# A decoder trunk in float32: one more projection in seven products, and low parts made by adding transfers

## The chip, the cores and the metric

The kernel runs on one core of one Trainium2 chip. The metric is the device time of one execution in microseconds (us); lower is better.

## The reference

A small decoder trunk works on 512 tokens of width 1024 (T = 512, D = 1024) in float32. There are two layers. Each layer is a half-step SwiGLU FFN, a mixer, and a second half-step FFN, each with an RMSNorm ahead of it:

```python
x = x + 0.5 * swiglu(rmsnorm(x, g1), wg, wu, wd)   # FFN: D -> 2816 -> D
x = x + mixer(rmsnorm(x, g2))                      # layer 0: gated linear attention, layer 1: stick-breaking attention
x = x + 0.5 * swiglu(rmsnorm(x, g3), wg, wu, wd)

def swiglu(h, w_gate, w_up, w_down):
    return (silu(h @ w_gate) * (h @ w_up)) @ w_down
```

So there are four FFNs, each with three products of 1024 x 2816 weights. The change touches the FFNs alone.

## The kernel before

**Precision.** TensorE multiplies rounded numbers (fp32r). Each operand v is therefore split into a high part h (v rounded, a ScalarE copy) and a low part l = v - h (a VectorE subtraction), and each product is three matmuls: h·h, l·h and h·l. For weights this is done in `Entry.split` (lines 127 and 129: tiles `wh` and `wl`, made from the loaded tile `raw`, or `rawd` for down). For activations it is done in `cut` (lines 783 and 784).

**Entries and the feed.** The work of TensorE is a list of entries, which `Feed` plays in order. When an entry starts, the weights of it and of the next two are split, the views of the next three are made (a view may compute sums of weight blocks), and the loads of the next five are issued on SyncE's queue. Within that, the instructions of each engine go out in the order in which they were scheduled at build time, and each engine works in that order. Weight tiles `wh` and `wl` have four buffers, `raw` has two, `rawd` has two, and the banks of the accumulator memory are eight.

**An FFN.** The 2816 hidden columns are 11 chunks of 256. Gate and up of a chunk are done in one of two ways. In the plain way (`feat`), an entry makes 128 columns out of 8 blocks of the input, with 24 matmuls of 512 columns. In the other way (`seven`), a chunk of 256 columns is made by a Strassen-like scheme over 2 x 2 halves, with seven products in place of eight: each is 12 matmuls of 256 columns, in two entries (`body_1`, `body_2`, line 689). It needs sums of weight blocks (`s12` and `s34`, lines 672 to 679), sums of input blocks T (`ts`, line 793, made in `normed_input` and split by `sums` into `th` and `tl`), and copies of partial sums out of the accumulators by ScalarE (z, o0, o1 and u3, lines 713 to 731), from which VectorE goes on. In every FFN chunk 0 and chunk 1 go the plain way in gate and in up, and chunks 2 to 10 are done with seven products.

**Down.** The chunks are in groups, and the down product of a group is done while the next group's gate and up run. A plain `down` entry takes 24 matmuls of 512 columns and adds into x from the accumulator (line 323, VectorE). One group of two chunks has its down done in seven products too (`seven_down`, line 368). There the accumulators are also read by VectorE's adds into x (line 374); the bank of the third product t3 goes on to take t4, after the add has read it.

**Start of an FFN.** The FFN begins before its RMSNorm is known: its first entries work on the gained but not normalised x, and their evacuations multiply by R, the reciprocal norm (lines 823 and 830). When R is known (lines 533 or 556), VectorE makes the normalised input (`xn`, `nl`, `ts`) in four pieces spread over the next entries; `NORMED` says from which entry on it is used. Then `sums` splits the eight sums T in pieces, which must be there before the first `seven`. The constants of this order are:

```python
GROUPS = ((0, 2), (2, 4), (4, 6), (6, 8), (8, 9), (9, 11))
NORMED, SEVEN, AHEAD = 6, 2, 2
DOWN_SEVEN = (1,)
SEVEN_UP = (2, 3, 4, 5, 6, 7, 8, 9, 10)
```

So ahead of the first `seven` there are eight plain entries (gate and up of chunks 0 and 1) and two of the four downs of group 0.

**GpSimd** has no part in the FFNs. It issues a few small loads for the mixers and the load of the last norm's gain.

Of the kernel before, what the change touches and what calls it, by code (L numbers as in the profile page):

```python
# [10 lines left out]
F32 = mybir.dt.float32  # L11
# [4 lines left out]
ALU = mybir.AluOpType  # L16
# [16 lines left out]
def decoder(ctx: ExitStack, tc: tile.TileContext, a: dict, out: bass.AP):  # L33
# [61 lines left out]
    class Entry:  # L95
# [3 lines left out]

        def __init__(self, units, body, place=0, lead=False):  # L100
            self.units, self.body, self.W, self.place = units, body, None, place
            self.lead, self.views = lead, None

        def view(self):

# [4 lines left out]
        def split(self):  # L110
            if self.W is None:
                self.W = []
                for r, (_, _, n, m) in zip(self.view(), self.units):
                    few = n * m < 1024
                    if few:

                        h = st["few"].tile([P, n * m + NEAR], F32R, tag="vh", bufs=1, name="wh")[:, NEAR:]
                        l = st["few"].tile([P, n * m + 64 - NEAR], F32R, tag="vl", bufs=1, name="wl")[:, : n * m]
                    else:
                        h, l = (  # L120
                            wp.tile([P, n * m + 64], F32R, tag="w" + t, bufs=4, name="w" + t)[
                                :, self.place : self.place + n * m
                            ]
                            for t in "hl"
                        )
                    h, l = (t.rearrange("p (n m) -> p n m", m=m) for t in (h, l))
                    st["cut"] = nc.scalar.copy(h, r).ins  # L127
                    with tc.issue_after(st["gains"]):
                        nc.vector.tensor_tensor(out=l, in0=r, in1=h.bitcast(F32), op=ALU.subtract)  # L129
                    self.W.append((h, l))  # L130
                    if self.lead and len(self.W) == 1:

                        first = wp.tile([P, P], F32R, tag="w1", bufs=1, name="w1")
                        nc.scalar.copy(first, r[:, 0, 0:P])
                        self.first = first
# [158 lines left out]

                feed.q.append(Entry([u], body))

    def down(w, r0, nf, hs, part, nxt, late=0):


        nd = KD // nf  # L300
        src = w[r0 : r0 + nf * P, part * nd * P : (part + 1) * nd * P]
        ch = Chunk(src.rearrange("(f p) c -> p f c", p=P), nf, nd * P)
        ch.few = True

        def body(W):
            (wh, wl), = W
            acc = []

            def prod(m, fs):
                if m == len(acc):  # L310
                    acc.append(psum("ps_d"))
                s = slice(m * P, (m + 1) * P)
                for f in fs:
                    mm3(acc[m], wh[:, f, s], wl[:, f, s], hs[f][0], hs[f][1], f == 0, f == nf - 1)

            if late:
                for m in range(nd):
                    prod(m, range(nf - late))
            for m in range(nd):
                prod(m, range(nf - late if late else 0, nf))  # L320
                ps = acc[m]
                k = part * nd + m
                nc.vector.scalar_tensor_tensor(  # L323
                    out=xs[k], in0=ps, scalar=0.5, in1=xs[k], op0=ALU.mult, op1=ALU.add
                )
                if nxt is not None:
                    nxt(k)
                yield

        feed.q.append(Entry([(ch, lambda t: t, nf, nd * P)], body))  # L330

    def seven_down(pool, w, r0, hs, part):

# [69 lines left out]
        def body_2(W):  # L403
            s, a22 = W
            ws, qs = v["w"], v["q"]
            for m in range(2):
                prod(ws[m], s, 0, 1, m, "t3", False)
                add(m, 1, 1, ws[m])
            yield
            for m in range(2):  # L410
                prod(qs[m], s, 2, 1, m, "b22", False)
                add(m, 0, 1, qs[m])
            yield
            for m in range(2):
                prod(ws[m], a22, 0, 1, m, "t4", False)
                add(m, 1, 0, ws[m])
            yield
# [168 lines left out]
    class FFN:  # L586
# [3 lines left out]

        GROUPS = ((0, 2), (2, 4), (4, 6), (6, 8), (8, 9), (9, 11))
        NORMED, SEVEN, AHEAD = 6, 2, 2
        DOWN_SEVEN = (1,)
        SEVEN_UP = (2, 3, 4, 5, 6, 7, 8, 9, 10)

        def __init__(self, wg, wu, wd, gi, nxt, first=False, last=False):
            self.gi, self.normed = gi, False
            self.after_ffn = bool(phases) and isinstance(phases[-1], FFN)  # L600
            self.defer, self.gates = [], []
            self.lead = []
            self.hs = [[] for _ in self.GROUPS]
            base, downs, late = len(feed.q), [], []
            self.sums_by = 10**6
            for group, (c0, c1) in enumerate(self.GROUPS):
                slots, put = 2 * (c1 - c0), 0
                if group == 1:

                    for put in range(self.AHEAD):  # L610
                        down(*downs[put], late=put == 0)
                    put = self.AHEAD
                for i in range(slots):
                    c, f = c0 + i // 2, i % 2
                    if f == 0:
                        g, u = Chunk(cols(wg, c * 256, 256), KD, 256), Chunk(cols(wu, c * 256, 256), KD, 256)
                    d = self.defer if i == 0 and c == 0 else None
                    f_ = f
                    if first and c == 0:

                        g, u = (Chunk(cols(w, f * P, P), KD, P) for w in (wg, wu))
                        self.lead += [g, u]
                        f_ = 0
                    if c >= self.SEVEN:
                        if f == 0:
                            self.sums_by = min(self.sums_by, len(feed.q) - base)
                            self.seven(g)
                    elif c not in self.SEVEN_UP:
                        feat(g, f_, self.evac_g, defer=d)
                    elif f == 0:  # L630
                        feat(g, 0, self.evac_g), feat(g, 1, self.evac_g)
                        self.sums_by = min(self.sums_by, len(feed.q) - base)
                    if c not in self.SEVEN_UP:
                        feat(u, f_, lambda ps, h=group: self.evac_u(ps, h), defer=d)
                    elif f == 1:
                        self.seven(u, group)

                    if late and i == 0:
                        seven_down(*late.pop())
                    while c >= self.SEVEN and put < len(downs) * (i + 1) // slots:  # L640
                        down(*downs[put])
                        put += 1
                    if group - 1 in self.DOWN_SEVEN and i == 1:
                        args = (lambda: self.tp, wd, self.GROUPS[group - 1][0] * 256, self.hs[group - 1])
                        seven_down(*args, 0)
                        late.append((*args, 1))
                for x in downs[put:]:
                    down(*x)
                n = 2 * (c1 - c0)
                end = group + 1 == len(self.GROUPS)  # L650
                downs = [(wd, c0 * 256, n, self.hs[group], part, nxt if end else None) for part in range(n)]
                if group in self.DOWN_SEVEN:
                    downs = []
            self.count = len(feed.q) - base
            if last:
                back_tok(wd, c0 * 256, n, self.hs[group], nxt)
            else:
                for x in downs:
                    down(*x)
            self.total = len(feed.q) - base  # L660
# [149 lines left out]
        def sums(self):  # L810
            def piece(i):

                h = np_.tile([P, T], F32R, tag="xh", name="th")
                l = np_.tile([P, T], F32R, tag="xl", name="tl")
                self.ts[i] = self.cut(h, l, self.ts[i].rearrange("p a b -> p (a b)"))


            return [lambda i=i: piece(i) for i in (0, 1, 2, 4, 6, 3, 5, 7)]
# [58 lines left out]
        def run(self, between=None):  # L877
            with tc.tile_pool(name="hp", bufs=8, reuse_waits="tile") as self.hp, tc.tile_pool(
# [20 lines left out]
                self.normed = True  # L899
                st["h"], st["l"] = zip(*self.n)  # L900
                todo = self.sums()
                spread(todo[:5], self.sums_by - self.NORMED)
                feed.entries(1, True)
                for piece in todo[5:]:
                    piece()
                feed.entries(self.count - self.sums_by - 1, True)
                if between is not None:
                    with tc.issue_after(st["silu"]):
                        nc.scalar.preload_act_table_set("sqrt_and_others")
# [681 lines left out]
```

## Time and profile before

| | |
|---|---|
| median of 3 runs | 1854.52 us (1854.33 to 1854.69) |
| the profiled execution, its own time | 1856.01 us |
| its span in the profile | 1854.0 us |
| granted TensorE clock | 0.999 |
| TensorE matmul, busy | 1828.8 us, 99%, 12187 matmuls |
| VectorE, busy | 1476.4 us, 80% |
| ScalarE, busy | 1035.9 us, 56% |
| GpSimd, busy | 8.7 us |

In the profile PE is TensorE's matmul, PEld its weight load, DVE VectorE, ACT ScalarE, POOL GpSimd and SP SyncE. A row of a group gives the source line, the engine, the operation, the tiles written and read, the shape, the count, the busy time, the mean duration in ns, and the idle time of the engine just before, with what ended it. A row of the timeline or of the chain gives the start in us, the length in us, the engine and the line. A row of waits gives who waited for whom, the total in us, how often and the longest.

### The profile page before, as it was taken

Reading aid. Unit: us, or ns where it says so; the run is one execution under the profiler, and the core shown is the slowest. Engines: PE = TensorE matmul, PEld = TensorE weight load, DVE = VectorE, ACT = ScalarE, POOL = GpSimd, SP = SyncE. Lnnn points to the kernel's source line nnn. Section 1 sums busy time; section 2 is a strip of 40 time slices with the busy share of each in tenths; the row PEclk is TensorE's granted clock in tenths of the full one; section 3 lists DMA queues with packets and bytes.
Section 4 is the critical chain, followed back from the end, with each engine's and each line's share of the span. In section 5 each row is a group of like instructions: output and inputs, shape, how many; then the busy total and the mean of one; then the engine's idle time right before and its main releaser. Section 6 shows DMA issues by size and latency. Waiting matters only on the chain.

```text
span 1854.0 us, 29888 instructions
## 1 busy us (share of the span) xinstructions
PE 1828.8 (99%) x12187; PEld 1649.6 (89%) x12187; DVE 1476.4 (80%) x2336; ACT 1035.9 (56%) x1771; POOL 8.7 (0%) x20
## 2 busy tenths in 40 slices
PE   7999999999999999999999999999999999999998
PEld 6999999889888899999889999998888788999997
DVE  7998776785787989877798997676878779997775
ACT  6555445444555565545565555455878755654454
POOL 0000000100000000000000000000000000000000
PEclk9999999999999999999999999999999999999999
DMA  5333333311223223332233333232221222333321
GB/s 160 114 125 95 118 110 100 98 57 62 69 69 114 91 92 115 115 114 87 82 128 104 98 118 107 95 92 85 69 69 59 67 91 93 112 125 97 121 80 69
DMA packets 177613, 179.16 MB, mean 97 GB/s; under 512 B 4098, under 2 KB 167988, under 8 KB 177476
## 3 DMA queue, kind: packets, MB, share of 16 engines
q1 hardware_dynamic: 176768, 176.18, 30.1%
q8 instruction: 95, 1.56, 0.4%
q0 software_dynamic: 608, 1.05, 0.2%
q14 instruction: 42, 0.34, 0.1%
q10 hardware_dynamic: 100, 0.03, 0.0%
HBM read 175.17 MB, written 2.10 MB: 96 GB/s over the span
## 4 chain that ended last, share of the span: by engine, by line
PE 86%; DVE 9%; DMA 3%; ACT 2%; issue 1%; SPq 0%; DVEq 0%; ACTq 0%
PE ps_d L67 20%; PE ps_f L67 18%; PE ps_w L689 17%; PE ps_q L689 9%; PE ps_t L67 5%; PE ps_z L689 4%; PE ps_b L67 4%; DVE wl L129 3%; DMA raw<-in_ffn_w_gate_dram 2%; PE ps_S L67 1%; PE ps_z L1315 1%; PE ps_bt L67 1%; PE ps_oT L1377 1%; PE ps_w L368 1%; DVE x L374 1%
## 5 line engine op out<-in xcount | busy, mean ns | idle before, releaser
L129 DVE TENSOR_TENSOR wl<-raw,wh 128x1024 fp32r<-128x1024 f32 (+1 forms) x244 | 259.2, 1066 | 89.3 <-ACT wh L127 50.1
L127 ACT CAST wh<-raw 128x1024 fp32r<-128x1024 f32 (+1 forms) x244 | 224.7, 923 | 160.4 <-PE ps_d L67 45.4
L689 PE MATMUL ps_w<-th,wh 128*128 128x256 f32 x864 | 239.6, 277 | 1.4 <-ACT o L719 0.6
L689 PE MATMUL ps_w<-tl,wh 128*128 128x256 f32 x864 | 238.7, 276 | 0.0
L689 PE MATMUL ps_w<-th,wl 128*128 128x256 f32 x864 | 238.6, 276 | 0.0
L129 DVE TENSOR_TENSOR wl<-s,wh 128x1024 fp32r<-128x1024 f32 x160 | 195.4, 1222 | 54.0 <-PE ps_z L689 37.4
L127 ACT CAST wh<-s 128x1024 fp32r<-128x1024 f32 x160 | 168.0, 1050 | 116.8 <-PE ps_d L67 28.9
L67 PE MATMUL ps_d<-hh,wl 128*128 128x512 f32 x544 | 212.1, 390 | 0.0
L67 PE MATMUL ps_d<-hh,wh 128*128 128x512 f32 x544 | 212.1, 390 | 0.0
L67 PE MATMUL ps_d<-hl,wh 128*128 128x512 f32 x544 | 211.6, 389 | 0.0
L67 PE MATMUL ps_f<-xh,wh 128*128 128x512 f32 x448 | 178.9, 400 | 1.6 <-ACT wh L127 1.6
L67 PE MATMUL ps_f<-xl,wh 128*128 128x512 f32 x448 | 175.8, 393 | 0.0
L67 PE MATMUL ps_f<-xh,wl 128*128 128x512 f32 x448 | 175.1, 391 | 0.0
L689 PEld LDWEIGHTS ps_w<-th,wh 128*128 128x128 f32 x864 | 162.3, 188 | 3.0 <-ACT u L731 1.0
L689 PEld LDWEIGHTS ps_w<-th,wl 128*128 128x128 f32 x864 | 162.2, 188 | 0.0
L689 PEld LDWEIGHTS ps_w<-tl,wh 128*128 128x128 f32 x864 | 162.2, 188 | 0.0
L127 ACT CAST wh<-rawd 128x1024 fp32r<-128x1024 f32 (+1 forms) x84 | 84.9, 1012 | 120.3 <-PE ps_d L67 77.4
L323 DVE SCALAR_TENSOR_TENSOR x<-ps_d,x 128x512 f32<-128x512 f32 x152 | 102.9, 688 | 58.6 <-PE ps_d L67 58.0
L129 DVE TENSOR_TENSOR wl<-rawd,wh 128x1024 fp32r<-128x1024 f32 (+1 forms) x84 | 98.3, 1174 | 42.4 <-ACT wh L127 25.1
L67 PEld LDWEIGHTS ps_d<-hl,wh 128*128 128x128 f32 x544 | 102.1, 188 | 21.6
L67 PEld LDWEIGHTS ps_d<-hh,wh 128*128 128x128 f32 x544 | 102.1, 188 | 20.2
L67 PEld LDWEIGHTS ps_d<-hh,wl 128*128 128x128 f32 x544 | 102.1, 188 | 19.7
(323 smaller groups left out, 4847.9 us busy)
## 6 DMA issues: line engine op xcount, KB each, us to landing
raw<-in_ffn_w_gate_dram SPq DMA_DIRECT2D x43, 1024.0 KB, 5.4
raw<-in_ffn_w_up_dram SPq DMA_DIRECT2D x43, 1024.0 KB, 5.4
rawd<-in_ffn_w_down_dram SPq DMA_DIRECT2D x84, 512.0 KB, 3.7
raw<-in_gla_w_in_dram SPq DMA_DIRECT2D x12, 1024.0 KB, 5.3
raw<-in_sb_w_in_dram SPq DMA_DIRECT2D x16, 512.0 KB, 3.8
raw<-in_gla_w_out_dram SPq DMA_DIRECT2D x4, 1024.0 KB, 5.0
raw<-in_sb_w_in_dram SPq DMA_DIRECT2D x4, 1024.0 KB, 5.1
raw<-in_sb_w_out_dram SPq DMA_DIRECT2D x4, 1024.0 KB, 5.0
```

Of the source, the lines that this page charges most:

```text
L67: st["pe"] = nc.tensor.matmul(ps, l, r, start=first, stop=last).ins
L127: st["cut"] = nc.scalar.copy(h, r).ins
L129: nc.vector.tensor_tensor(out=l, in0=r, in1=h.bitcast(F32), op=ALU.subtract)
L323: nc.vector.scalar_tensor_tensor(out=xs[k], in0=ps, scalar=0.5, in1=xs[k], op0=ALU.mult, op1=ALU.add)
L368: st["pe"] = nc.tensor.matmul(ps, l_, r_, start=first and c + n == 0, stop=c == 1 and n == 2, skip_group_check=True).ins
L374: nc.vector.scalar_tensor_tensor(out=x, in0=ps, scalar=0.5, in1=x, op0=ALU.mult, op1=ALU.add)
L689: st["pe"] = nc.tensor.matmul(o, l_, r_, start=first and j + n == 0, stop=j == 3 and n == 2, skip_group_check=True).ins
L1315: nc.tensor.matmul(o_, l_, r_, start=first, stop=last, skip_group_check=True)
L1377: nc.tensor.matmul(po[e * 64 : e * 64 + 64, j * P : T], self.v[j][:, c : c + 64], self.wt[p, e][bk][:, c0 : c0 + n], start=j == 0, stop=j ...
```

## The change

1. Up of chunk 1 is done with seven products (`SEVEN_UP` from 1 on). Its gate stays plain.
2. The groups' borders move from 2, 4, 6, 8, 9 to 1, 3, 5, 7, 9. The group of a single chunk is now chunk 0, not chunk 8, and the group whose down is done in seven products is chunks 3 and 4, not 2 and 3.
3. Both downs of chunk 0 stand between the two plain gate entries of chunk 1. Ahead of the first `seven` there are now five plain entries, the two downs and one more plain entry. The four pieces of the normalised input are spread over three entries, not four, and the eight pieces of T's splitting over the three entries after that (six) and just ahead of the first `seven` (two).
4. The low part of these two downs' weights and of T is made without VectorE: ScalarE writes -v into the tile of l, rounded as h is, and a transfer on GpSimd's queue adds v to it, which leaves v - h.
5. In the seven-product down, ScalarE copies the accumulator after t3 into a tile `u3`, and VectorE adds into x from the copy.

```diff
@@ Entry.split
                     st["cut"] = nc.scalar.copy(h, r).ins
+                    if self.adds:
+
+                        nc.scalar.activation(l, r, AF.Copy, scale=-1.0)
+                        nc.gpsimd.dma_start(out=l, in_=r, accum_op=ALU.add)
+                        self.W.append((h, l))
+                        continue
                     with tc.issue_after(st["gains"]):
                         nc.vector.tensor_tensor(out=l, in0=r, in1=h.bitcast(F32), op=ALU.subtract)
@@ down: adds=False as a new argument, at the end
         feed.q.append(Entry([(ch, lambda t: t, nf, nd * P)], body))
+        feed.q[-1].adds = adds
@@ seven_down, body_2
+            u3 = pool().tile([P, 2, H], F32, tag="c", bufs=1, name="u3")
             for m in range(2):
                 prod(ws[m], s, 0, 1, m, "t3", False)
-                add(m, 1, 1, ws[m])
+                nc.scalar.copy(u3[:, m], ws[m])
+                add(m, 1, 1, u3[:, m])
@@ FFN
-        GROUPS = ((0, 2), (2, 4), (4, 6), (6, 8), (8, 9), (9, 11))
-        NORMED, SEVEN, AHEAD = 6, 2, 2
-        DOWN_SEVEN = (1,)
-        SEVEN_UP = (2, 3, 4, 5, 6, 7, 8, 9, 10)
+        GROUPS = ((0, 1), (1, 3), (3, 5), (5, 7), (7, 9), (9, 11))
+        NORMED, SEVEN = 5, 2
+        DOWN_SEVEN = (2,)
+        SEVEN_UP = (1, 2, 3, 4, 5, 6, 7, 8, 9, 10)
@@ FFN.__init__
-                if group == 1:
-
-                    for put in range(self.AHEAD):
-                        down(*downs[put], late=put == 0)
-                    put = self.AHEAD
...
                     elif f == 0:
-                        feat(g, 0, self.evac_g), feat(g, 1, self.evac_g)
+                        feat(g, 0, self.evac_g)
+
+                        for put, x in enumerate(downs):
+                            down(*x, late=put == 0, adds=True)
+                        downs = []
+                        feat(g, 1, self.evac_g)
                         self.sums_by = min(self.sums_by, len(feed.q) - base)
@@ FFN.sums
-                self.ts[i] = self.cut(h, l, self.ts[i].rearrange("p a b -> p (a b)"))
+                t = self.ts[i].rearrange("p a b -> p (a b)")
+                nc.scalar.copy(h, t)
+
+                nc.scalar.activation(l, t, AF.Copy, scale=-1.0)
+                nc.gpsimd.dma_start(out=l, in_=t, accum_op=ALU.add)
+                self.ts[i] = h, l
@@ FFN.run
-                spread(todo[:5], self.sums_by - self.NORMED)
-                feed.entries(1, True)
-                for piece in todo[5:]:
+                spread(todo[:6], self.sums_by - self.NORMED)
+                for piece in todo[6:]:
                     piece()
-                feed.entries(self.count - self.sums_by - 1, True)
+                feed.entries(self.count - self.sums_by, True)
```

More of the change, by code (lines that the diff above doesn't have):

```diff
@@ L101, in __init__ @@
             self.units, self.body, self.W, self.place = units, body, None, place
-            self.lead, self.views = lead, None
+            self.lead, self.views, self.adds = lead, None, False
         def view(self):
@@ L295, in back, with down @@
                 feed.q.append(Entry([u], body))
-    def down(w, r0, nf, hs, part, nxt, late=0):
+    def down(w, r0, nf, hs, part, nxt, late=0, adds=False):
         nd = KD // nf
```

## The prediction

> **What bounds the kernel now.** I read the page first (busy shares, then the chain that ended last), then the chain in order of time for the spacing of the matmuls, then the waits.
>
> ```profile
> span 1854.0 us, 29888 instructions
> PE 1828.8 (99%) x12187; PEld 1649.6 (89%) x12187; DVE 1476.4 (80%) x2336; ACT 1035.9 (56%) x1771; POOL 8.7 (0%) x20
> PE 86%; DVE 9%; DMA 3%; ACT 2%; issue 1%; SPq 0%; DVEq 0%; ACTq 0%
> ```
>
> TensorE is busy for 99% of the span and owns 86% of the chain. Since ends of matmuls are modelled, I check it by starts. The next rows are from the chain in order of time: start, length, what, how many; the two before them give the shapes.
>
> ```profile
> L67 PE MATMUL ps_f<-nh,wh 128*128 128x512 f32 x64 | 24.9, 389 | 0.0
> L689 PE MATMUL ps_w<-th,wl 128*128 128x256 f32 x864 | 238.6, 276 | 0.0
> 290.88 2.72 PE ps_w L689 x24
> 353.50 10.88 PE ps_f L67 x48
> 598.79 34.98 PE ps_f L67 x154
> 633.77 10.88 PE ps_d L67 x48
> ```
>
> The 24 products of 256 columns take 2.72 us, 113.3 ns each, and the 48 of 512 columns take 10.88 us, 226.7 ns each: the same price per column, with starts so close that "mean ns of one" (276, 389) is overlap. In the second FFN the plain products run on for 34.98 us without a pause and the down products follow at once. So here TensorE's work is the time, almost to the last microsecond, and what is taken from it is gained. The Trainium skill ("Trainium Kernel Development and Optimization", Performance Expectations, Reading a trace) says that matmul busy time tells badly how near a kernel is to its limit and that the share of weight loading tells better. By that rule the 89% would leave 11% that better feeding could win; the even spacing of the starts speaks against it here, and the sum below goes by the starts.
>
> What is left of waiting inside the FFNs is in the waits of TensorE and of its weight loads: us in total, times, longest.
>
> ```profile
> PE ps_w L368 <- DVE x L374: 5.4, 8, 1.1
> PE ps_w L689 <- ACT o L719: 0.6, 1, 0.6
> PE ps_w L689 <- ACT u L731: 0.4, 2, 0.2
> PE ps_w L689 <- ACT ps_z L713: 0.4, 2, 0.2
> PEld ps_w L368 <- DVE x L374: 7.2, 9, 1.3
> ```
>
> **Edit 1, chunk 1's up in seven products.** Each of the four FFNs gives up two plain up entries, 48 products of 512 columns, 10.88 us. It gains 7 x 4 x 3 = 84 products of 256 columns, 84 x 113.3 ns = 9.52 us. That is 1.36 us less per FFN and 5.4 us in all, on the engine that sets the time. Nothing else of TensorE's work changes: the group of one chunk, with its eight sums into x, moves from chunk 8 to chunk 0, and the number of down products stays.
>
> **Edit 2, the sum in down copied by ScalarE.** After the t3 product, TensorE needs the bank again for t4, and VectorE has to have read it. VectorE stands in a long subtraction then, so TensorE waits: 5.4 us in eight places, one for each half of each FFN's seven-product down (7.2 us as the weight loads see it). The seven products of gate and up do already what the edit does, and the wait on their copy (u, L731) is 0.4 us over 72 of them. So the gain is bounded by 7.2 us and by nothing at all, if VectorE's lateness only comes out at the next operand that it has to make. I take 5.4 us: VectorE keeps its adds, but none of them stands between two products any more, and the copies lie on ScalarE, at 56%.
>
> **Edit 3, the order.** Group borders are now 1, 3, 5, 7, 9. The last two chunks get four downs between their sevens where they had two, and the seven-product down comes after two chunks with a down behind every seven. Both give VectorE more TensorE time to hide behind. The waits that could go are 0.6 + 0.4 + 0.4 = 1.4 us; I take half, 0.7 us, with 0 and 1.4 as ends.
>
> **Edit 4, the start of each FFN, where the price lies.** So far eight plain entries and two downs stood ahead of the first seven (in the second FFN it starts at 633.77 + 10.88 = 644.65). Now eight entries do (five plain, two downs, one plain), so it starts 10.88 us earlier after the same beginning, at 633.8. The normalised input and the sums T must be ready by then. The windows show what VectorE has to spare: us, then busy time of PE, PEld, DVE, ACT.
>
> ```profile
> 600.00:610.00 10.00, 10.00 (x46) 8.26 (x45) 9.10 (x16) 7.13 (x10) 0.00 (x0) 1.00 0.00 0
> 610.00:620.00 10.00, 10.00 (x46) 8.29 (x45) 10.00 (x21) 6.51 (x11) 0.00 (x0) 1.00 0.01 2
> 620.00:630.00 10.00, 10.00 (x46) 8.24 (x45) 10.00 (x17) 8.02 (x15) 0.00 (x0) 1.00 0.46 137
> 630.00:640.00 10.00, 10.00 (x46) 8.29 (x45) 9.93 (x15) 2.29 (x4) 0.00 (x0) 1.00 0.56 179
> 640.00:650.00 10.00, 10.00 (x70) 9.22 (x69) 10.00 (x15) 4.06 (x6) 0.00 (x0) 1.00 0.34 105
> 30.00:40.00 10.00, 10.00 (x46) 8.28 (x45) 10.00 (x20) 6.03 (x9) 0.00 (x0) 1.00 0.00 2
> 938.00:948.00 10.00, 10.00 (x46) 8.29 (x45) 10.00 (x20) 7.46 (x10) 0.00 (x0) 1.00 0.00 0
> 1529.00:1539.00 10.00, 10.00 (x46) 8.29 (x45) 10.00 (x20) 6.81 (x11) 0.00 (x0) 1.00 0.00 1
> ```
>
> VectorE has nothing to spare: 49 of 50 us, and the same at that place in the other three FFNs, though no wait of TensorE comes of it yet. So I count what must be done in the shorter time. VectorE's instructions overlap, and the timeline gives the distance of their starts:
>
> ```profile
> 602.25 0.69 DVE L556 SCALAR_TENSOR_TENSOR R<-v,R 128x512 f32<-128x512 f32 x1
> 602.86 1.22 DVE L129 TENSOR_TENSOR wl<-raw,wh 128x1024 fp32r<-128x1024 f32 x1
> 605.19 1.41 DVE L777 SCALAR_TENSOR_TENSOR xn<-x,gT,R 128x512 f32<-128x512 f32 x2
> 606.51 0.42 DVE L793 TENSOR_TENSOR ts<-xn 128x256 f32<-128x256 f32 x1
> 608.65 0.69 DVE L784 TENSOR_TENSOR hl<-t,hh 128x512 fp32r<-128x512 f32 x1
> 609.26 0.42 DVE L793 TENSOR_TENSOR ts<-xn,ts 128x256 f32<-128x256 f32 x1
> 609.59 0.42 DVE L793 TENSOR_TENSOR ts<-xn 128x256 f32<-128x256 f32 x1
> 644.73 1.23 DVE L129 TENSOR_TENSOR wl<-s,wh 128x1024 fp32r<-128x1024 f32 x1
> 645.87 0.68 DVE L673 TENSOR_TENSOR s<-s,raw 128x512 f32<-128x512 f32 x1
> ```
>
> A 512-wide one costs 0.60 (608.65 to 609.26), a 256-wide one 0.33, a 1024-wide one 1.14, a pair of xn 1.32. R is there at 602.9. The second product of the first seven, which reads T and s12, comes at 633.77 + 1.36 = 635.1, so VectorE has 32.2 us. Its list: the low part in hand 1.14; chunk 0's eight evacuations 4.8; four normalised pieces, each 1.32 + 2 x 0.60 + 4 x 0.33 = 3.84, 15.4; the first gate of chunk 1, 0.6; the low parts of the two plain gate entries 2.3; two sums and two low parts for the seven 3.5; eight sums of the downs into x, 4.8. Together 32.5 us. It fits to within 0.3 us, but only because T's eight low parts (4.8) and those of the two downs (2.3) have left VectorE: with them the list is 39.6 us, and TensorE would stand still for 7 us in each FFN. What can be late next is any pause of VectorE in that list: the windows show 0.9 us of pause at its head. I take 0.5 us per FFN, 2 us in all; the ends are nothing, where a few of the downs' sums slip behind the seven, and 3 us per FFN, 12 us.
>
> **Edit 5, the transfers that add.** The low part is now -t written by ScalarE, and a transfer on GpSimd's queue that adds t: ten more ScalarE passes per FFN (8 at 0.62, 2 at 1.05: 7.1 us on an engine that is busy for 28 of these 50 us) and ten transfers. Nothing of before adds in a transfer; the nearest rows are plain ones of that queue; rows of VectorE and ScalarE stand with them:
>
> ```profile
> lf<-in_c_lvl_dram POOLq DMA_DIRECT2D x1, 224.0 KB, 2.7
> fin<-in_final_norm_dram POOLq DMA_DIRECT2D x1, 512.0 KB, 4.1
> 332.12 1.95 POOL L988 DMA_DIRECT2D w<-in_gla_w_gk_dram  x4
> 332.90 1.23 DVE L129 TENSOR_TENSOR wl<-rawd,wh 128x1024 fp32r<-128x1024 f32 x1 [0.36 <-ACT wh L127]
> L783 ACT CAST th<-ts 128x512 fp32r<-128x512 f32 x32 | 17.8, 616 | 0.3 <-DVE ts L793 0.3
> L127 ACT CAST wh<-s 128x1024 fp32r<-128x1024 f32 x160 | 168.0, 1050 | 116.8 <-PE ps_d L67 28.9 <-DVE s L679 26.9 <-PE ps_q L689 20.4
> ```
>
> Four were issued in 1.95 us, so ten cost GpSimd some 5 us, and it has no other work in an FFN. For T's 256 KB I bound the landing from below by 2.7 us (224 KB) and from above by 8.2, twice the 512 KB row, since an add must read its target too; I take 4, near that row itself. If T's last two pieces are written about 626, where the windows above still have VectorE full, ScalarE needs 4 x 0.62 = 2.5 us and the transfer 4: 632.5. The piece read last among the even ones is needed at 635.1 + 0.9, the odd ones at the fifth product, 639.2. So 3.5 us are over, and I cost the edit at nothing. That cover is gone from 7.5 us of landing on; at the upper bound it would cost 0.7 us per FFN, 2.8 us in all, which the range holds. Behind a late transfer stand the tiles it reads, which VectorE's next sums for the sevens reuse, and the weight buffer's next load on SP's queue. The Trainium skill ("SBUF — State Buffer", summary rules) advises against hiding a GpSimd-issued transfer under VectorE, because making its descriptors starves while VectorE runs in a two-port mode. By that rule the issues would stretch by the subtractions beside them, up to 1.2 us each. The trace does not agree for these subtractions: the one at 332.90 ran beside the four issues, which kept 0.49 us each.
>
> **The sum.** 5.4 + 5.4 + 0.7 - 2.0 = 9.5 us less. The profiled execution took 1856.01 us, so 1846.5; it lay 1.5 us above the median of the runs (1854.52), which gives 1845.0.
>
> **Rivals.** (a) Slower: the transfers come one behind another instead of overlapping. First T pieces leave ScalarE about 611 (the first sums are done at 609.6); eight at 4.1 us land by 644, against the 636 allowed: 8 us per FFN, 32 in all, and the total is 1845.0 + 32 = 1877. The gain is gone once the wait per FFN exceeds (9.5 / 4) = 2.4 us, that is from (636 - 611 + 2.4) / 8 = 3.4 us for each transfer. For it: no row shows an adding transfer, and issues held up by VectorE would act the same way. Against: the four small ones overlapped. Chance 0.18. (b) VectorE's start of the FFN costs its upper end, 12 us: 10 us later than forecast, 1855, no change. For it: full windows. Against: the list fits. Chance 0.07. (c) Edit 2 does not do what it says, since VectorE's lateness comes out elsewhere: 5.4 us less gain, 1850.4; with (b) half true it is 1852 or more. Chance 0.13, of which half ends within the bound below. (d) All goes well: 5.4 + 7.2 + 1.4 = 14 us less, 1840.5. Chance 0.10. The forecast, between 1841 and 1850, has 0.52.
>
> **How the numbers follow.** A measurement of this kernel can tell 0.2%, 3.7 us, from no change. Faster: forecast, (d) and half of (c), 0.68. Same: (b) and the rest of (c), 0.14. Slower: (a), 0.18. The range goes from 1840 (d) to 1855 (b) and leaves out (a); the forecast's own range is 1841 to 1850.
>
> **What would show it.** TensorE's products of 512 columns fall by 4 x 48 and those of 256 rise by 4 x 84; the wait of ps_w (L368) on VectorE's x vanishes, with a small one on the new copy; the first seven of each FFN starts 10.9 us sooner after its R. Wrong would be: waits of TensorE on tl or on a transfer there (then a), on wl or nl (then b), or on wl in the seven-product down (then c).

## The result and the profile after

The changed kernel takes 1864.92 us (median of 6 runs, 1863.49 to 1869.16) against 1854.61 us for the kernel before beside it (6 runs): 1.006 of the time before, 95% interval 1.0047 to 1.0072. That is 10.3 us slower, where 9.5 us faster had been forecast. The profiled execution took 1866.02 us, its span 1864.2 us.

The page of the kernel after, its rows of busy time, the chain's shares, and two groups of TensorE by form:

```profile
span 1864.2 us, 30434 instructions
PE 1830.6 (98%) x12331; PEld 1657.3 (89%) x12331; DVE 1467.4 (79%) x2332; ACT 1075.1 (58%) x1859; POOL 43.2 (2%) x60
PE 86%; DVE 8%; DMA 4%; ACT 2%; issue 1%; SPq 0%; DVEq 0%; ACTq 0%
L67 PE MATMUL ps_f<-nh,wh 128*128 128x512 f32 x32 | 12.4, 389 | 0.0
L699 PE MATMUL ps_w<-th,wl 128*128 128x256 f32 x912 | 252.5, 277 | 0.0
```

TensorE has 144 matmuls more and is still at 98%, so this part of the page does not show what happened. Counted by form over the whole trace, those of 256 columns went from 7648 to 7984 (+336) and those of 512 from 3734 to 3542 (-192): at 113.3 and 226.7 ns that is 5.4 us less work. The span grew by 10.2 us all the same, so TensorE stood still for longer. The waits say at whom (us in total, times, longest):

```profile
PE ps_w L699 <- ACT ps_z L723: 6.8, 7, 2.3
PE ps_w L699 <- ACT u L741: 5.5, 7, 1.7
PE ps_q L375 <- ACT o L709: 3.2, 2, 1.7
PE ps_w L375 <- ACT ps_z L393: 0.2, 1, 0.2
ACT wh L127 <- DVE s L689: 23.9, 5, 6.4
DVE s L688 <- DMA tl<-ts: 7.4, 3, 2.5
DVE s L682 <- DMA raw<-in_ffn_w_gate_dram: 17.5, 19, 1.9
ACT w L140 <- DMA raw<-in_ffn_w_up_dram: 13.6, 8, 2.7
```

The 5.4 us that TensorE waited for VectorE's x in the seven-product down are gone. In their place it waits for small ScalarE copies (z, u, o), and these are only the last link: ScalarE waits for VectorE's sums, and VectorE for a transfer (`tl<-ts`) and for weight loads.

To place the stalls I add up, entry by entry, how far the starts of TensorE's matmuls are apart beyond 113.3 ns or 226.7 ns each. Two places hold them: the start of each FFN, up to the end of its first four projections in seven products (two entries each), and the stretch, the six entries from the first to the last one of the seven-product down.

| us of stall, four FFNs together | before | after |
|---|---|---|
| the start | 1.3 | 13.0 |
| the stretch | 10.8 | 13.7 |

**The start.** In the second FFN of the kernel after, the timeline of GpSimd, SyncE, VectorE, ScalarE and TensorE (start, length, what, and the idle time before it with its cause):

```profile
626.25 0.85 POOL L829 DMA_DIRECT2D tl<-ts  x1 [2.68 <-DVE t L838]
627.81 0.86 POOL L829 DMA_DIRECT2D tl<-ts  x1 [0.71 <-ACT tl L828]
627.24 0.37 SPq L92 DMA_DIRECT2D raw<-in_ffn_w_gate_dram  x1
635.57 0.69 DVE L688 TENSOR_TENSOR s<-raw 128x512 f32<-128x512 f32 x1 [2.53 <-DMA tl<-ts]
636.96 1.05 ACT L127 CAST wh<-s 128x1024 fp32r<-128x1024 f32 x1 [6.41 <-DVE s L689]
639.33 0.37 ACT L723 COPY ps_z<-ps_w 128x256 f32<-128x256 f32 x1
639.76 0.38 PE L699 MATMUL ps_w<-th,wh 128*128 128x256 f32 x1 [2.30 <-ACT ps_z L723]
```

From the bottom up: TensorE waits 2.30 us for a copy of an accumulator. ScalarE makes that copy late because, ahead of it in its order, stands the high part of a weight sum for which it has waited 6.41 us. VectorE makes that sum late because the sum's tile is one of the four buffers that T used (tag `s`), and the sixth transfer, issued at 627.81, still reads from it. That transfer landed at 635.5, 7.7 us after its issue. The DMA view of two windows, 605 to 626 us and 625 to 640 us (count, KB each, median us from issue to landing), shows what ran beside it:

```profile
tl<-ts POOLq DMA_DIRECT2D x4, 256.0 KB, 5.3
...
tl<-ts POOLq DMA_DIRECT2D x4, 256.0 KB, 7.9
raw<-in_ffn_w_gate_dram SPq DMA_DIRECT2D x1, 1024.0 KB, 7.1
```

Of the four in the second window the first landed in 4.0 us; the three that were issued behind the 1 MB weight load (627.24) took 7.7 to 8.3 us. In the third FFN the first five land in 3.3 to 4.0 us and the last three, beside that load, in 7.5 to 9.1 us.

A part of the start's stalls is not waiting. Right behind this pause the granted clock falls to half for 3.4 us (window, its length, TensorE's busy time and products, granted clock, DMA share, GB/s):

```profile
634.00:637.00 3.00, 3.00 (x26) 1.00 1.08 196
640.50:643.50 3.00, 3.00 (x16) 0.50 0.40 134
```

The products of 256 columns start 213 ns apart there, not 113, which makes 1.6 of the 13.0 us. The starts of the other three FFNs of this run have no such spell.

**The stretch.** In the third FFN the chain through the seven-product down reads (start, length, what):

```profile
1118.33 7.38 DMA raw<-in_ffn_w_gate_dram
1125.79 0.69 DVE s L682
1126.49 0.34 DVE o L745
1126.86 0.04 ACT o L709
1128.11 1.65 PE ps_q L375 x12
```

The gate's load is late, the sum over it is late, an evacuation behind the sum is late, and the banks that the next product wants come free late. In the kernel before, the same pair of loads (a 512 KB one for down, and 0.6 us behind it a 1 MB one) landed the second in 5.9 to 6.1 us in seven of eight places of this stretch. In the kernel after, four of eight took 6.9 to 8.0 us.

### The profile page after: what moved, and what is told of

It reads as the page before. It is cut to its first block, busy times and chain, and to the rows that moved or that the text cites. A ratio compares the mean times of both kernels' runs of the same rounds, so it can differ in the third digit from the quotient of the medians.

```text
span 1864.2 us, 30434 instructions
## 1 busy us (share of the span) xinstructions
PE 1830.6 (98%) x12331; PEld 1657.3 (89%) x12331; DVE 1467.4 (79%) x2332; ACT 1075.1 (58%) x1859; POOL 43.2 (2%) x60
## 4 chain that ended last, share of the span: by engine, by line
PE 86%; DVE 8%; DMA 4%; ACT 2%; issue 1%; SPq 0%; DVEq 0%; ACTq 0%
PE ps_d L67 20%; PE ps_w L699 17%; PE ps_f L67 16%; PE ps_q L699 8%; PE ps_t L67 5%; PE ps_b L67 5%; PE ps_z L699 4%; DVE wl L135 3%; DMA raw<-in_ffn_w_gate_dram 2%; PE ps_w L375 2%; PE ps_S L67 1%; PE ps_z L1329 1%; PE ps_bt L67 1%; DMA raw<-in_ffn_w_up_dram 1%; PE ps_oT L1391 1%
## 5 line engine op out<-in xcount | busy, mean ns | idle before, releaser
L135 DVE TENSOR_TENSOR wl<-raw,wh 128x1024 fp32r<-128x1024 f32 x244 | 256.1, 1053 | 102.1 <-ACT wh L127 68.3
L699 PE MATMUL ps_w<-th,wh 128*128 128x256 f32 x912 | 254.4, 279 | 12.4 <-ACT ps_z L723 6.8
L699 PE MATMUL ps_w<-tl,wh 128*128 128x256 f32 x912 | 252.6, 277 | 0.0
L699 PE MATMUL ps_w<-th,wl 128*128 128x256 f32 x912 | 252.5, 277 | 0.0
L699 PEld LDWEIGHTS ps_w<-th,wh 128*128 128x128 f32 x912 | 171.7, 188 | 15.8 <-ACT ps_z L723 8.4
L699 PEld LDWEIGHTS ps_w<-tl,wh 128*128 128x128 f32 x912 | 171.6, 188 | 0.0
L67 PE MATMUL ps_f<-xh,wh 128*128 128x512 f32 x416 | 166.5, 401 | 0.5 <-ACT wh L127 0.5
L67 PE MATMUL ps_f<-xl,wh 128*128 128x512 f32 x416 | 163.3, 392 | 0.0
L67 PE MATMUL ps_f<-xh,wl 128*128 128x512 f32 x416 | 162.6, 391 | 0.0
L135 DVE TENSOR_TENSOR wl<-rawd,wh 128x1024 fp32r<-128x1024 f32 (+1 forms) x76 | 88.2, 1165 | 27.5 <-ACT wh L127 18.2
```

Of the source, the lines that this page charges most:

```text
L67: st["pe"] = nc.tensor.matmul(ps, l, r, start=first, stop=last).ins
L699: st["pe"] = nc.tensor.matmul(o, l_, r_, start=first and j + n == 0, stop=j == 3 and n == 2, skip_group_check=True).ins
```

## The experiments

First theories: **A**, a transfer of T lands late and holds T's buffer, behind it VectorE, ScalarE (both in order) and TensorE. **B**, the shortened start does not hold VectorE's list. **C**, edit 2 saves nothing, its waits only move. The runs come from four occasions, on which the kernel before took 1853.4 to 1854.6 us, so medians of different occasions compare to about 1 us; the ratio is to the kernel before of the same occasion. Of the runs below, the table gives the median, the ratio to the kernel before with its interval, the stalls in the two places, and how many of the eight paired 1 MB loads of the stretch took 6.7 us or more (profile of each run).

| run | us | ratio | start | stretch | slow loads |
|---|---|---|---|---|---|
| before | 1853.4 to 1854.6 | 1 | 1.3 | 10.8 | 1 |
| after | 1864.92 | 1.0060 (1.0047 to 1.0072) | 13.0 | 13.7 | 4 |
| e1 before, edit 2 alone | 1849.32 | 0.9971 (0.9960 to 0.9982) | 0.2 | 5.6 | 0 |
| e2 after, no edit 2 | 1869.40 | 1.0081 (1.0066 to 1.0096) | 13.9 | 17.7 | 4 |
| e3 after, T's low parts by VectorE | 1867.49 | 1.0075 (1.0058 to 1.0091) | 14.5 | 12.3 | 4 |
| e4 after, T in another order | 1856.56 | 1.0013 (1.0003 to 1.0022) | 5.2 | 11.8 | 4 |
| e5 after, no edit 1 | 1857.76 | 1.0021 (1.0011 to 1.0030) | 10.7 | 5.8 | 1 |
| e6 before, T's transfers alone | 1878.33 | 1.0136 (1.0121 to 1.0151) | 25.2 | 10.1 | 2 |
| e7 e4, seven-product down later | 1848.74 | 0.9973 (0.9963 to 0.9982) | 4.6 | 6.5 | 2 |
| e8 e4, pieces 5 and 7 by VectorE | 1853.48 | 1.0002 (0.9992 to 1.0011) | 3.2 | 10.6 | 4 |
| e9 after, instructions shifted | 1862.93 | 1.0051 (1.0034 to 1.0068) | 13.9 | 4.4 | 0 |
| e10 before, instructions shifted | 1863.69 | 1.0055 (1.0040 to 1.0070) | 0.6 | 13.0 | 2 |
| e11 e7 and e8 | 1849.62 | 0.9979 (0.9970 to 0.9988) | 3.2 | 8.6 | 4 |
| e12 e11, instructions shifted | 1852.19 | 0.9993 (0.9984 to 1.0002) | 2.1 | 6.6 | 1 |

**Edit 2, alone and left out (e1, e2).**

```diff
@@ e1: the kernel before; e2 is the reverse, on the kernel after
+            u3 = pool().tile([P, 2, H], F32, tag="c", bufs=1, name="u3")
-                add(m, 1, 1, ws[m])
+                nc.scalar.copy(u3[:, m], ws[m])
+                add(m, 1, 1, u3[:, m])
```

> The kernel before, with edit 2 alone: ScalarE copies the sum after t3, VectorE adds from the copy. Theory C (VectorE and the weight loads set the pace of the stretch around the seven-product down, and the waits on its adds were only the place where that showed): the waits on the adds go, others of like size come within the same stretch, and the time stays within 2 us of before. Rival (the prediction's term): 5 us faster, with under 1 us of new waits.

> The changed kernel with edit 2 alone undone: VectorE adds from the accumulator again. Theory C: within 2 us of the changed kernel, since the stretch loses about 14 us of TensorE's time either way over the four FFNs. Rival 1 (edit 2 works, and its 5 us are eaten elsewhere): 4 to 6 us slower than the changed kernel. Rival 2 (the copies on ScalarE are what made the stretch worse): 3 us or more faster than the changed kernel.

Alone it takes 5.0 us off the kernel before; left out of the kernel after it costs 4.5 us. The wait on VectorE's x comes back in e2 (its waits):

```profile
PE ps_w L375 <- DVE x L381: 4.8, 8, 1.2
```

So C falls: edit 2 is worth what the prediction said, in both surroundings.

**T's low parts (e3, e4).** e3 gives T's eight subtractions back to VectorE. e4 changes one line, so that the buffers come free in the order in which the sums want them:

```diff
@@ e4
-            return [lambda i=i: piece(i) for i in (0, 1, 2, 4, 6, 3, 5, 7)]
+            return [lambda i=i: piece(i) for i in (0, 1, 2, 3, 4, 6, 5, 7)]
```

> The changed kernel with T's low parts made by VectorE's subtraction again, the two downs' low parts still by transfers. Theory A (the transfers' landing holds the buffers of T, VectorE waits for them at the sums of the first seven, and ScalarE behind it): VectorE has 4.8 us more to do per FFN but waits 2.4 us less, so the stalls at the first sevens stay near 3 to 5 us per FFN and the time within 6 us of the changed kernel, with no wait of VectorE on a transfer. Theory B (the start is too short for VectorE's list, and the transfers are not what counts): 4 x 4.8 = 19 us slower than the changed kernel.

> The changed kernel with one tuple altered: T's pieces are split in the order 0, 1, 2, 3, 4, 6, 5, 7 instead of 0, 1, 2, 4, 6, 3, 5, 7, so that the buffer which the first seven's second sums need is let go by the fourth transfer, not by the sixth, and before the weight load that runs beside the last three. Nothing is left out. Theory A: VectorE's wait of 2.4 us on the transfer goes in FFNs 2 to 4, the stalls at the first sevens fall from 13 us to 5 or less, and the time is 6 to 9 us below the changed kernel. Theory B: unchanged within 2 us.

e4 takes 8.4 us off the kernel after, and the waits have none of VectorE on a transfer. The sum that stood at 635.57 in the kernel after, after a wait of 2.53 us, follows without one in e4 (VectorE's timeline, same FFN):

```profile
630.58 0.68 DVE L688 TENSOR_TENSOR s<-raw 128x512 f32<-128x512 f32 x1
```

The last transfers are as slow there (7.8 and 8.0 us), but nobody waits for the buffers that they hold. That is A. The cover is thin: in the third FFN the chain of e4 still runs through one of them (8.5 us), and 5.2 us of stalls are left at the start. e3, 2.6 us slower than the kernel after, is far from B's 19 us, but shows that B has a share: with no transfer of T at all the start stalls as long, 14.5 us, now on VectorE's own products:

```profile
PE ps_w L699 <- ACT o L729: 4.5, 4, 1.1
PE ps_w L699 <- DVE wl L135: 3.2, 4, 0.9
```

The shortened start holds neither: T by VectorE costs 3.6 us per FFN, T by transfers in the wrong order 3.3 us.

**Is it the length of the start? (e5, e6)** e5 gives the start its 10.9 us back; e6 puts T's transfers into the kernel before.

```diff
@@ e5, on the kernel after (downs and their order kept)
-        SEVEN_UP = (1, 2, 3, 4, 5, 6, 7, 8, 9, 10)
+        SEVEN_UP = (2, 3, 4, 5, 6, 7, 8, 9, 10)
@@ e6, on the kernel before
-                self.ts[i] = self.cut(h, l, self.ts[i].rearrange("p a b -> p (a b)"))
+                nc.scalar.copy(h, t)
+                nc.scalar.activation(l, t, AF.Copy, scale=-1.0)
+                nc.gpsimd.dma_start(out=l, in_=t, accum_op=ALU.add)
```

> The kernel after, with edit 1 alone undone: chunk 1's up again in eight plain products, so TensorE gets 5.4 us of work back over the four FFNs and the start of each is 10.9 us longer again; the eight transfers of T, down's transfers, their order and edit 2 all stay. Theory A (a transfer that lands late costs only because the short start takes away what hid it): the stalls of the start, 13.0 us in the profile after, fall under 2 us, and the time is 1864.9 + 5.4 - 11 to 13, 1857 to 1860 us. Rival E (the late transfers hold T's buffers and so VectorE and ScalarE whatever the start's length): the stalls stay near 13 us and the time is near 1870 us.

> The kernel before, with T's low parts by adding transfers as in the kernel after, in before's order of pieces and before's order of entries, nothing else. Theory A: the start is long enough, the time is the kernel before's within 2 us (1852.5 to 1856.5 us). Rival E (the transfers hold VectorE and ScalarE whatever the start's length): 8 to 12 us more, near 1864 us. VectorE loses eight subtractions per FFN here, which no theory takes to be on the path.

A missed e5's stalls and e6's time. e5's time lies where A put it, but for another reason: the wait on a transfer is gone, and the start still stalls for 10.7 us, now on a late gate load (8.7 us in the second FFN, beside the last transfers of T and the load for up); what fell was the stretch, 13.7 to 5.8 us. e6 costs 25 us, more than twice what Rival E gave. Its waits show the same chain with another victim:

```profile
DVE s L678 <- DMA tl<-ts: 17.7, 4, 6.0
ACT hh L783 <- DVE t L836: 22.0, 7, 6.9
PE ps_d L67 <- ACT hh L783: 14.9, 4, 4.6
```

There the sum that wants T's buffer stands in VectorE's list ahead of an evacuation that the first downs wait for, and the transfers, beside two 1 MB and two 512 KB loads, take 6.0 to 8.4 us each in the third FFN. About 6 of e6's 25 us of stalls are products at half clock, in four spells (3.4 to 6.8 us) at its pauses. So a longer start alone does not cover a late transfer; what counts is what stands behind the buffer in VectorE's list. Of the theory, the chain stays and the condition falls.

**The stretch (e7, e8).** After e4 most of the start's share was explained, the stretch's was not. Theory **D**: the chunks whose weights are loaded there make the loads slow. Rival **F**: the lateness is left over from the start.

```diff
@@ e7, on e4
-        DOWN_SEVEN = (2,)
+        DOWN_SEVEN = (3,)
@@ e8, on e4: pieces 5 and 7
+                if i in (5, 7):
+                    nc.vector.tensor_tensor(out=l, in0=t, in1=h.bitcast(F32), op=ALU.subtract)
+                else:
```

> The kernel after with T's pieces in the order of the fourth experiment (0, 1, 2, 3, 4, 6, 5, 7) and with the seven-product down moved from group 2 (chunks 3, 4) to group 3 (chunks 5, 6); as much work as there. The fourth experiment took 1856.6 us, with 11.9 us of stalls around the seven-product down, where the kernel before with edit 2 alone had 5.9 us in the same place and the same instructions around it, but its weight loads there landed in 5.8 to 6.2 us and not 6.9 to 7.5 us. Theory D (it is which chunks' weights are loaded side by side in that stretch that makes the loads slow): with other chunks the loads land in about 6 us, the stalls fall to about 6 us, and the time to about 1850.5 us. Rival F (the lateness comes from what the changed start and the changed order of downs leave behind, or from all chunks being alike): stalls near 12 us, time near 1856.5 us.

> The fourth experiment (the kernel after with T's pieces in the order 0, 1, 2, 3, 4, 6, 5, 7), and the last two pieces, 5 and 7, by VectorE's subtraction in place of a transfer. Theory A (the last transfers, which fall beside the 1 MB weight load, land late and hold a buffer): the stalls of the start fall from 5.4 us in the fourth experiment to 2 to 3 us, and the time from 1856.6 to 1853.5 to 1855 us. Rival B (VectorE's list is the limit at the start, so each subtraction put back is paid): two subtractions more in each of four FFNs, 3 us more and over, 1859 us or above.

e8 goes the way that A says: the start falls to 3.2 us and the time by 3.1 us (2.1 when each run is taken against the kernel before of its occasion), and no transfer of T is left on its chain. But the gate load beside them is also faster, 5.2 to 7.9 us in the four FFNs where e4 has 7.0 to 9.3, and e8 does not tell the two apart. e7 takes 7.8 us off e4 (6.9 in the same way) and 4.6 us off the kernel before, just as D says, but two of its eight loads were still slow (6.8 and 7.2 us), and e5 had kept the chunks and lost all slow loads but one. D did not fit that.

**Theory G: TensorE's own instructions (e9, e10).** Section 3 of the page of the kernel after lists the queues (packets, MB, share of 16 engines):

```profile
q1 hardware_dynamic: 176768, 176.18, 29.8%
q0 software_dynamic: 6368, 13.64, 4.1%
q8 instruction: 96, 1.57, 0.4%
```

96 packets of 16 KB for 12331 matmuls is one for 128. The Trainium skill ("Runtime: NRT & Kernel Launch", Instruction fetch mechanics) says that an engine's instructions are refilled in blocks of 16 KiB, 256 instructions, over a DMA queue that its sequencer drives itself, and calls the cost mostly hidden. By that rule 12331 matmuls and as many weight loads make 96.3 blocks; the trace agrees with its 96 packets. Whether the cost is hidden is another matter. Each packet takes 0.9 to 1.8 us, and the DMA view of the window 1117 to 1126 us of the kernel after, which holds the late pair above, has one:

```profile
q8 instruction: 1, 0.02, 1.0%
raw<-in_ffn_w_gate_dram SPq DMA_DIRECT2D x1, 1024.0 KB, 7.4
rawd<-in_ffn_w_down_dram SPq DMA_DIRECT2D x1, 512.0 KB, 5.2
```

To move the packets and leave loads, buffers and order as they are, I put unused matmuls ahead of TensorE's first one, where it waits 6 us for data:

```diff
@@ e9: n = 27, on the kernel after; e10: n = 33, on the kernel before; e12: n = 18, on e11
+        for _ in range(n):
+            nc.tensor.transpose(ps[:, P : 2 * P], ident, ident)
         nc.tensor.transpose(ps[:, 0:P], gl, ident)
```

> The kernel after, with 27 transposes of the identity put ahead of the first instruction of TensorE's program (into a part of a PSUM tile that nobody reads; TensorE waits there for the first data anyway for 6 us). Nothing else is touched: same loads, same buffers, same order. Theory G: TensorE's instructions arrive in packets of 16 KB on a queue of their own, one packet per 128 matmuls (96 packets for 12331 matmuls in the profile after, each about 1.1 us), and a 1 MB weight load issued 0.6 us behind a 512 KB one lands late (6.8 to 8.0 us and not 5.8 to 6.2) where such a packet falls 0.9 to 3.0 us behind the pair's first issue: 19 of 19 such pairs in the nine profiles so far. 27 matmuls more move each packet about 3 us forward, which takes it away from the pairs of the first three FFNs that it hits in the profile after (1.6, 1.1, 2.0 us; the fourth, 2.8, stays near the edge): those loads land in about 6 us, the stalls around the seven-product down fall from 13.8 to 8 to 10 us, and the time by 4 to 6 us, to 1859 to 1862 us. Theory D (which chunks' weights are loaded makes them slow) and Rival F (lateness left by the start): nothing moves, 1864 to 1867 us with the start's transposes.

> The control the other way: the kernel before, with 33 transposes of the identity ahead of TensorE's first instruction and nothing else changed. Of the pairs of loads around its seven-product down, three have a packet 5.8 to 6.0 us behind their first issue (second to fourth FFN) and land in 5.9 to 6.1 us; 33 matmuls move the packets 3.7 us forward, to 2.1 to 2.3 us. The first FFN's pair that took 7.9 us (packet at -0.6 us) loses its packet. Theory G: the three loads take about 7.2 us, the first FFN's about 6 us; the stalls there grow by 1 to 2 us in each of the three and shrink by about 2 us in the first. Theory D: all loads as in the kernel before. The transposes themselves may put off the first product by up to 2.5 us; so the time is 1856 to 1860 us by theory G and 1854 to 1857 us by theory D, and the loads tell the two apart, not the time.

In e9 all eight loads of the stretch land in 5.8 to 5.9 us, and the stretch's stalls fall from 13.7 to 4.4 us, further than expected. The same window as above, now of e9, with the same pair of loads:

```profile
q1 hardware_dynamic: 1568, 1.57, 53.2%
issues: line engine op xcount, KB each, median us to landing
raw<-in_ffn_w_gate_dram SPq DMA_DIRECT2D x1, 1024.0 KB, 5.9
rawd<-in_ffn_w_down_dram SPq DMA_DIRECT2D x1, 512.0 KB, 3.6
```

The time is another matter: 1862.93 us is over the range that theory G gave, and the ratios of the two kernels, 1.0051 and 1.0060, have intervals that overlap. The opening differs: the first product comes at 18.95 us in place of 15.83, and the granted clock shows two spells of 3.4 us at half speed, one ahead of it and one that begins with it. From the first product to the end, the profiled execution takes 1840.6 us against 1848.4, 7.8 us less.

In e10 two of the three loads named became slow (7.4 and 7.3 us), the packets at 1.7 and 2.1 us behind the pair; in the third the packet went further than counted, to 0.8 us ahead, and the load stayed at 5.9. The first FFN's 7.9 us load fell to 5.9. The stalls moved with them: 3.9 to 3.0 (less of a fall than expected), 2.3 to 4.3, 2.2 to 2.1 and 2.4 to 3.7 us in the four FFNs. One pair in the second FFN of e10 (window 709.5 to 718 us):

```profile
q8 instruction: 1, 0.02, 0.6%
raw<-in_ffn_w_up_dram SPq DMA_DIRECT2D x1, 1024.0 KB, 7.4
```

Its time, 10 us over the kernel before, is above both expectations. The two profiled executions are 6.5 us apart, and that can be placed: 5.2 us are the later first product and 2.2 us the stretch, with 0.7 us less at the start. The rest of the 10 us lies outside the traces, because the profiled execution of e10 was the fastest of its four (1862.36 us) and that of the kernel before lay 2.4 us above the median beside e10 (1856.01 against 1853.57 us).

D and F fall as the cause of these slow loads, since every load, buffer and order stayed in both kernels. Over the fourteen profiles there are 156 such pairs. In 28 the packet starts 0.8 to 4.0 us behind the pair's first issue, and all 28 loads took 6.8 to 8.0 us. Of the other 128, 119 took less than 6.7 (median 5.9). For the other nine (6.7 to 7.9) I have no cause; in three of them a packet had started 0.5 to 0.6 us ahead of the pair. The bounds are read off these same profiles (the expectation of e9 had 0.9 to 3.0 us), and no packet started between 4.1 and 5.5 us behind a pair or between 0.4 us ahead of one and 0.7 us behind it, so the true bounds stay open. By this account e7 gained because fewer packets fell on its stretch, and not by its chunks; no run moved its packets alone, so for e7 it is inferred.

**Towards a better kernel (e11, e12).**

> Towards a better kernel: the kernel after with T's pieces in the order 0, 1, 2, 3, 4, 6, 5, 7, pieces 5 and 7 by VectorE's subtraction, and the seven-product down in group 3 (the seventh and eighth experiments together). Those took 8 us less (1848.7 against 1856.6) and 3 us less (1853.5) than the fourth. If they add up: 1845.5 to 1847 us, 0.4% faster than the kernel before. If VectorE's two subtractions more are paid where the stretch no longer hides them: 1848 to 1850 us.

> The same kernel with 18 transposes of the identity ahead of TensorE's first instruction. In the seventh experiment packets of instructions fell 0.9 and 1.0 us behind the pairs of the second and the fourth FFN, whose loads took 6.8 and 7.2 us; 18 matmuls move them 2 us forward, to before the pairs, and leave the others at 3.8 us and more. Theory G: these two loads take about 6 us, and the time is 2 to 4 us under the run without the transposes. Theory D: the same as without.

In e11 the two gains do not add up: the start falls from e7's 4.6 to 3.2 us, but its stretch has four loads of 6.7 us and more and stalls for 8.6 us, not 6.5. The time is e7's within its spread. It lies in the range that was given for paying VectorE's subtractions, but the trace shows the slow loads in their place; two of the four have no packet in the window above. In e12 the two loads named land in 5.8 and 6.0 us; another, with its packet now 4.0 us behind, takes 7.1. From the first product on it is the shortest (1830.6 us against e11's 1832.8), but the start takes back 3.6 us, so it missed its expectation. e7 (1848.74 us), e1 (1849.32 us) and e11 (1849.62 us) beat both kernels; their intervals overlap, so none of them is shown to be the best.

## Why the prediction was wrong

- **Edit 1** was right: 5.4 us less work on TensorE, by the counts, and the first seven stands about 10.9 us nearer to the FFN's first product, as forecast.
- **Edit 2** was right: 5.4 us forecast, 5.0 and 4.5 measured. Rival (c) is out.
- **Edit 3**: the stalls behind the stretch, in the last groups, fell by 1.0 us (0.7 forecast).
- **Edits 4 and 5** failed, by 2 us forecast against 11.7 us of stalls. Edit 4 made a list of VectorE's work and called it fitting, though it came to 32.5 us for 32.2; and the list does not hold pauses. Edit 5 took 4 us for a landing and said that cover lasts until 7.5 us. The size was right for a transfer by itself (3.3 to 4.0 us) and wrong beside a 1 MB load (7.5 to 9.1 us). The larger fault is the use that the cover was reckoned for: TensorE's reading of T. The first to want something from a late transfer was VectorE, for the tile that it reads. The prediction names those tiles ("which VectorE's next sums for the sevens reuse") and gives them no price, nor does it look in which order the pieces free them. Rival (a) had the sign and the wrong mechanism: the transfers overlapped, and the order was most of the fault (13.0 us of stalls against 5.2 in e4). None of the waits named as signs of being wrong appeared (TensorE on tl, wl or nl): TensorE waited for ScalarE's copies.
- **Not in the sum**: the stretch. Edit 2 left 5.6 us of stalls there (e1); the kernel after has 13.7. The 8.1 us between them go with the four slow loads, and e9 takes 9.3 us away by shifting the instructions. No edit aimed at this, and where the packets fell was luck: in the kernel before none started 0.8 to 4.0 us behind a pair of the stretch, in the kernel after four did.

Together, with edit 2 by its stalls (10.8 to 5.6 us): -5.4 - 5.2 - 1.0 + 11.7 + 8.1 = +8.2 us. The profiled execution's first product is also 1.7 us later (15.83 against 14.14 us), which makes 9.9 of the 10.2 us between the spans; in other runs with the same opening it lies between 13.3 and 15.1 us.

The prediction also weighed the rule of the Trainium skill ("SBUF — State Buffer", summary rules) against hiding a GpSimd-issued transfer under VectorE in a two-port mode. No trace here shows the issues stretch: two issues in e6 with VectorE idle throughout took 0.86 us, and the 364 of all runs with VectorE busy for nine tenths of their time and more took 0.86 us in the median (0.85 to 1.00). They are longer than the small plain ones' 0.49 us. Whether VectorE's operations ran in such a mode, no run shows.

## What to carry to other kernels

When work moves from an engine to a transfer, price the buffers that the transfer holds as well as the result that it brings: ask who next wants the tile that it reads, what stands behind that one in its engine's order, and issue the pieces in the order in which the buffers are wanted. Price the landing beside the loads that run at that time, not by itself. In a kernel whose loads have little slack, a change in the number of TensorE's instructions also moves its instruction packets, and several us can come or go that belong to no edit; shift the packets before crediting or blaming an edit for them.

## What the runs showed of the hardware

- A transfer of 256 KB within on-chip memory that adds takes 3.3 to 4.0 us at best, up to 5.9 us where others of its kind or loads overlap a part of it, and 6.0 to 10.5 us beside large loads. GpSimd's issue of one takes 0.86 us.
- A 16 KB instruction packet of TensorE, about 1.1 us on its queue, delays a 1 MB load by 0.9 to 2.1 us if it starts 0.8 to 4.0 us behind the first issue of a pair of loads. A 1 MB load that is not one of a pair hardly feels it: median 5.4 us with a packet in its time, 5.3 us without, over the fourteen profiles. Where packet and load get in each other's way, the traces do not show.
- After the first 25 us, eight pauses of TensorE, over all runs, lasted 2.5 to 4.8 us. At seven of them (one in the kernel after, e2 and e5 each, four in e6) the granted clock then was at half for 3.4 or 6.8 us; at one (2.7 us, in e9) it stayed full. The one in the kernel after cost 1.6 us.
- With 18 to 33 transposes ahead of TensorE's first instruction, the first product came 3.1 to 5.2 us later, and the clock was at half for 3.4 to 10.2 us in the first 23 us. Three runs without them (e3, e5, e8) have 3.4 us of half clock there too, so the spells may not be the transposes' doing.
